# The second gate and the second up projection as three fp32r matmuls over split operands

## The chip, the cores and the metric

The kernel runs as one program on one core of a Trainium2 chip. The metric is device microseconds of one execution. Three timed runs of the kernel before gave 1217.91, 1217.97 and 1218.64 us, median 1217.97. One further execution was profiled, and all rows below are from that one. The chip's engines are named as the profile names them: PE (TensorE matmuls) and PEld (its weight loads), DVE (VectorE), ACT (ScalarE), POOL (GpSimd) and SP (SyncE, which here issues nearly all DMAs).

## The reference, cut to what matters

One layer over 256 tokens of width 1024, with 16 meta tokens set ahead of them. A mixer with an attention branch and a state space branch is followed by a mixture of 32 experts, each token to its best 4.

```python
g_a = jax.nn.sigmoid(proj[..., GA_OFF:GB_OFF])      # proj = h @ w_in
g_b = jax.nn.sigmoid(proj[..., GB_OFF:IN_COLS])
merged = g_a * (y_a @ w_up_a) + g_b * (y_b @ w_up_b)
return merged @ w_o
...
for e in range(N_EXPERTS):
    gate = jnp.minimum(t @ w_gate[e] + b_gate[e], SWIGLU_LIMIT)
    up = jnp.clip(t @ w_up[e] + b_up[e], -SWIGLU_LIMIT, SWIGLU_LIMIT)
    act = (up + 1.0) * gate * jax.nn.sigmoid(SWIGLU_ALPHA * gate)
    out = out + comb[:, e:e + 1] * (act @ w_down[e] + b_down[e])
```

g_b is the second gate (1024 x 1024 weights, 272 rows of h of which 256 count), y_b @ w_up_b the second up projection (512 x 1024 weights). All inputs are float32. The experts' three matrices are 12 MB each expert, 384 MB in all.

## The kernel before, in words

The work falls into a front (norm, projections, attention, scan, gates, output projection, router) and the expert loop, which goes over 16 pairs of experts. The order of PE and of SP is that of the program text (a manual schedule); the order of ACT, DVE and POOL is written by a planner that simulates the program and takes, among the instructions that it holds for ready, the one of highest priority. `tc.high_priority` raises that priority.

Weights come in tiles of 1 MB (128 partitions x 2048 float32). In the front they go through pool `wA` (6 tiles), and two further pools, `wC` and `wB`, are laid over memory that the front gives back: `wC` over that of the attention, `wB` over that of the scan. A fixed list, `slots` (20 homes; the first round, `first`, has 21), says into which home each quarter matrix of an expert goes. SP issues the loads in that order and waits at each one until the home's last reader is done. `prefetch(n)` issues the next n of them ahead of the expert loop. So at the start of the expert loop up to 21 MB of weights lie in SBUF, and from then on each load waits for a home to be used up.

`project` (line 214) is 8 matmuls of a 128 x 128 weight piece against 256 columns of hT, in float32. `gate_tile(i, hf_, j)` calls it for gate i, half hf_ and column block j, and ACT puts the result through tanh (L744). `up` (L764) is 4 such matmuls. The order of the front on PE around the change is: gate 0 (8 tiles), the up projection `up_a` d = 0 to 3, gate 1 tiles (0, 0) and (0, 1), up_a 4 and 5, gate 1 tiles (0, 2) and (0, 3), up_a 6 and 7, gate 1 tiles (1, 0) to (1, 3), the glu projection (4 times `up`), 32 transposing matmuls of hT into the output sums (L832), `up` of w_up_b for d = 0 to 7, then the output projection (L935) for the first and second half of the tokens, the latter mixed with the router, and the first gather. Two DVE instructions for each d (L839, L840) turn up_b's sums into mT, which the output projection reads.

The experts' gate and up biases are split into three bfloat16 pieces: rows are loaded three times (`braw`, six DMAs, L788), copied to `bias` by ACT (L789), and three times subtracted by DVE and copied by ACT (L792, L793), over all 2048 columns at once. The experts' loop uses them at L1064, and the home `acc` is the memory of `braw`.

Of the kernel before, what the change touches and what calls it, by code (L numbers as in the profile page):

```python
# [30 lines left out]
NS = 64  # L31
NPAIR = NG // 2
NE = 32
NWA, NWB, NWC = 6, 7, 5
NLEV = 9
HP = 120
CH = T // 2
# [11 lines left out]
def hybrid_trunk_kernel(ctx: ExitStack, tc: tile.TileContext, x, meta, ln_in_g, ln_in_b, w_in, b_f,  # L49
# [47 lines left out]
    def slab(src, kt):  # L97

        n = src.shape[1]
        src = src.rearrange("(k p) n -> p k n", p=P)  # L100
        nk, ks = 2048 // n, []
        for k0 in range(0, kt, nk):
            v_ = wA.tile([P, 2048], F32, name="w", tag="w").rearrange("p (k n) -> p k n", n=n)
            nc.sync.dma_start(v_, src[:, k0:k0 + nk])
            ks += [v_[:, k] for k in range(nk)]
        return ks

    def wslice(c0):
        return slab(w_in[0, :, c0:c0 + 512], KD)
# [101 lines left out]
    def project(w, j, n0, n1):  # L211
        pt = pst(n1 - n0)
        for k in range(KD):
            TE.matmul(pt, w[k][:, j * P:(j + 1) * P], hT[:, k, n0:n1], start=k == 0, stop=k == KD - 1)  # L214
        return pt
# [474 lines left out]

    moe = ExitStack()
    wC = moe.enter_context(tc.tile_pool(name="wC", bufs=NWC, reuse_waits="tile"))
    pools = {"wA": wA, "wC": wC, "fk": fk, "keep": keep}
    ready = {}
    nload = [0]
    slots = [("wC", "w")] * NWC + [("wB", "w")] * (NWB - 4) + [("wA", "w")] * NWA + [("keep", "gate1")]
    slots += [("wB", "w")] * 4 + [("fk", "hT")]
    first = slots[:NWC + NWB + NWA - 3] + [("keep", "acc")] + slots[NWC + NWB + NWA - 3:]

    def homes():  # L700

# [29 lines left out]
    def prefetch(n):  # L731
        seq = [(w, e, qtr) for e in range(2) for w in (w_gate, w_up) for qtr in range(4)]
        seq += [(w_down, e, qtr) for qtr in range(4) for e in range(2)]
        for _ in range(n):
            w, e, qtr = seq[nload[0]]
            ready[(w.tensor.name, e, qtr)] = expert_load(w, e, qtr)
# [3 lines left out]

    gate = [keep.tile([P, KD, SEQ], F32, name=f"gate{i}", tag=f"gate{i}") for i in range(2)]

    def gate_tile(i, hf_, j):
        S.activation(gate[i][:, 4 * hf_ + j], project(wg[2 * i + hf_], j, NMETA, T), AF.Tanh, scale=0.5)  # L744

    gate_tile(0, 0, 0)
    scan_out(5)
# [7 lines left out]
    scan_out(6)  # L755
    gate_tile(0, 1, 2)
    gate_tile(0, 1, 3)
    wg.append(wslice(GB_OFF))
    prefetch(2)

    def up(w, y, d):
        pt = pst(SEQ)
# [10 lines left out]
    scan_out(7)  # L773
    up_a(2)
    up_a(3)
    wg.append(wslice(GB_OFF + 512))
    scan.close()
    bp = moe.enter_context(tc.tile_pool(name="bp", bufs=1, side="right"))
    mk = front.enter_context(tc.tile_pool(name="mk", bufs=2, side="right"))
# [6 lines left out]
    for j, src in enumerate((b_gate, b_up)):  # L786
        for g in range(3):
            nc.sync.dma_start(braw[NE * g:NE * g + NE, j], src[0])  # L788
    S.copy(bias, braw)  # L789
    for g in (1, 2, 2):  # L790
        gs = slice(NE * g, NE * g + NE)
        V.tensor_tensor(braw[gs], braw[gs], bias[gs], ALU.subtract)  # L792
        S.copy(bias[gs], braw[gs])  # L793
    pick = keep.tile([3 * NE, NE], BF16, name="pick")
    with nc.allow_low_precision(reason="sums of zeros and a one"):
        V.tensor_reduce(pick, ident[:3 * NE, :3 * NE].rearrange("p (b e) -> p e b", e=NE), AX.X, ALU.add)
# [14 lines left out]
    for j in range(4):  # L811
        gate_tile(1, 1, j)
    prefetch(NWB - 4)
    wub = slab(w_up_b[0], 4)


    bh = mk.tile([P, 4], F32, name="bh")
# [1 line left out]
    for j in range(4):  # L819
        pt = up(wg_, y2T, j)  # L820
        tg = mk.tile([P, SEQ], F32, name="tg", tag="tg")
        S.activation(tg, pt, AF.Tanh, scale=0.25, bias=bh[:, j:j + 1])
        V.scalar_tensor_tensor(ybT[:, j], tg, 1.0, y2T[:, j], op0=ALU.add, op1=ALU.mult)


    po = [pw.tile([P, 2, 512], F32, name="po", tag="po"), [pst(512), pst(512)]]
# [5 lines left out]
            TE.matmul(pt, hT[:, k, ts], ident, start=k % 4 == 0, stop=False, skip_group_check=True)  # L832

    mT = fk.tile([P, KD, SEQ], F32, name="mT", tag="hT")
    prefetch(NWA)
    for d in range(KD):
        pt = up(wub, ybT, d)
        m2 = mk.tile([P, SEQ], F32, name="m2", tag="m2")
        V.scalar_tensor_tensor(m2, gate[1][:, d], 1.0, pt, op0=ALU.add, op1=ALU.mult)  # L839
        V.scalar_tensor_tensor(mT[:, d], m2, 0.125 / ALPHA, gate[0][:, d], op0=ALU.mult, op1=ALU.add)  # L840
# [178 lines left out]
    def weights(p, sel):  # L1019
        V.tensor_mul(sel, sel, bc(comb[:, :, 2 * p:2 * p + 2], 3, CAP))  # L1020
        pt = px.tile([P, 512], F32, name="px", tag="px")
        for i in range(2):
            TE.transpose(pt[:, i * P:(i + 1) * P], sel[:, i].rearrange("p e s -> p (e s)"), ident)
        selT = mp.tile([P, SEQ], F32, name="selT", tag="selT", bufs=2)
        S.copy(selT, pt[:, :SEQ])
        if p + 1 == NE // 2:

            pt = px.tile([P, 512], F32, name="px", tag="px")
            for i in range(2):
                for g in range(2):  # L1030
                    TE.matmul(pt[64 - 64 * g:128 - 64 * g, i * P:(i + 1) * P], sel[:, i, g], ident,
                              start=True, stop=True, skip_group_check=True)
            selX.append(mp.tile([P, SEQ], F32, name="selX"))
            S.copy(selX[0], pt[:, :SEQ])
        return selT

# [112 lines left out]
    def crowded():  # L1149

        anyc = nc.values_load(cnti[0:1, NE:NE + 1], min_val=0, max_val=SEQ)
        with tc.If(anyc > CAP):  # L1152
# [1 line left out]
            for s_ in home[nload[0] - 8:nload[0]]:  # L1154
                free.remove(s_)
            free = [s_ for s_ in free if s_[0] != "keep"]
            free.sort(key=lambda s_: ("wC", "fk", "wB", "wA").index(s_[0]))

            def slot(n):
                pool, tag = free[n]  # L1160
# [8 lines left out]
            with tc.For_i(0, NE, 1) as e:  # L1169
                ce = nc.values_load(cnti[0:1, bass.ds(e, 1)], min_val=0, max_val=SEQ)  # L1170
                with tc.If(ce > CAP):
                    def weights_of(w, n):
                        ts = []
                        for qtr in range(4):
                            ts.append(slot(n + qtr).rearrange("p (k n) -> p k n", n=D))
                            nc.gpsimd.dma_start(ts[-1], w[0, bass.ds(e, 1), qtr * 256:qtr * 256 + 256]
                                              .rearrange("o (k p) n -> p (o k) n", p=P))
                        return ts

                    scr = slot(1)  # L1180
                    a, sg, br, bu = scr[:, 0:512], scr[:, 512:1024], scr[0:1, 1024:], scr[32:33, 1024:]
                    nc.gpsimd.dma_start(br, b_gate[0, bass.ds(e, 1), :])
                    nc.gpsimd.dma_start(bu, b_up[0, bass.ds(e, 1), :])
                    aT = slot(2).rearrange("p (k t) -> p k t", k=KD)
                    wg_e, wu_e = weights_of(w_gate, 3), weights_of(w_up, 7)
                    for i in range(2):
                        for n in range(2):
                            ns = slice(n * 512, n * 512 + 512)
                            pts = []
                            for ws, bb_, r, tag in ((wg_e, br, 0, "pg"), (wu_e, bu, 32, "pu")):  # L1190
                                pt = pg.tile([P, 512], F32, name=tag, tag=tag)
                                TE.matmul(pt, ones[r:r + 1, 0:P], bb_[:, ns], start=True, stop=False)
                                for k in range(KD):
                                    TE.matmul(pt, h1Td[:, k, i * P:(i + 1) * P], ws[k // 2][:, k % 2, ns],
                                              start=False, stop=k == KD - 1)
                                pts.append(pt)
                            V.tensor_scalar_min(a, pts[0], 7.0)
                            S.activation(sg, a, AF.Sigmoid, scale=1.702)
                            V.tensor_mul(sg, sg, a)
                            V.tensor_scalar(a, pts[1], 7.0, -7.0, op0=ALU.min, op1=ALU.max)  # L1200
                            V.scalar_tensor_tensor(a, a, 1.0, sg, op0=ALU.add, op1=ALU.mult)
                            pt = px.tile([P, 512], F32, name="px", tag="px")
                            for j in range(4):
                                TE.transpose(pt[:, j * P:(j + 1) * P], a[:, j * P:(j + 1) * P], ident)
                            V.tensor_copy(aT[:, 4 * n:4 * n + 4, i * P:(i + 1) * P],
                                          pt.rearrange("p (k t) -> p k t", k=4))
                    wd_e = weights_of(w_down, 7)
                    for i in range(2):
                        for n in range(2):
                            ns = slice(n * 512, n * 512 + 512)  # L1210
                            pt = px.tile([P, 512], F32, name="px", tag="px")
                            for k in range(KD):
                                TE.matmul(pt, aT[:, k, i * P:(i + 1) * P], wd_e[k // 2][:, k % 2, ns],
                                          start=k == 0, stop=k == KD - 1)
                            V.scalar_tensor_tensor(acc[:, i, ns], pt, over[:, i, bass.ds(e, 1)], acc[:, i, ns],
                                                   op0=ALU.mult, op1=ALU.add)
# [147 lines left out]
```

## Time and profile before

| | before |
|---|---|
| median of 3 runs (lowest, highest) | 1217.97 us (1217.91, 1218.64) |
| the profiled execution: time, span of its instructions | 1219.16 us, 1217.6 us |
| mean granted TensorE clock over the span | 0.983 |
| PE busy, DVE busy, ACT busy | 1123.3, 334.8, 177.1 us |
| read from HBM | 431.64 MB, mean 355 GB/s over the span |

A profile is read in slices of time. [...] A timeline row has the start in us, the length from the start of the first to the end of the last instruction that it merges, the engine, the line of the kernel, the operation with out<-in, the shapes and the count; idle time before it and what ended it stand in brackets. Matmuls are pipelined and each one's length includes the way through the array, so the pace of a stream is read from the start of one row to the start of the next.

### The profile page before, as it was taken

What the parts mean: (1) busy time and instruction counts of PE and PEld (TensorE: products, weight loads), DVE (VectorE), ACT (ScalarE), POOL (GpSimd) and SP (SyncE); (2) the same over time, 40 slices, a digit from 0 to 9 for tenths busy, and PEclk for the clock granted to TensorE, in tenths of its full rate; (3) what the DMA queues carried; (4) which work ended last, traced back from release to release, by engine and by line L of the source; (5) the groups of instructions that cost most, each with busy time, mean ns of one, the idle gap of its engine ahead of it and who ended that gap; (6) DMA issues with size and microseconds to landing.
All of it is one profiled execution on the core that took longest, in us unless ns stands there. A gap on an engine that the chain in (4) does not pass through costs nothing. (4 is left out here: it accounts for less than half of the span.)

```text
span 1217.6 us, 13190 instructions
## 1 busy us (share of the span) xinstructions
PE 1123.3 (92%) x5398; PEld 579.7 (48%) x5399; DVE 334.8 (27%) x781; ACT 177.1 (15%) x387; POOL 59.0 (5%) x115
## 2 busy tenths in 40 slices
PE   4889999998999999999999999988999899988994
PEld 2778788853545444443444353424343344333431
DVE  3969422233121212111131312121212121212003
ACT  2257403021101011010101010101010111000000
POOL 3333200000000000000000000000000000000001
PEclk9999999998999999999999999999999999999998
DMA  7743289557999999999999999999999999999993
GB/s 151 187 103 71 105 206 385 229 205 303 392 421 420 421 421 421 421 421 409 421 421 421 421 421 421 421 421 420 421 420 421 422 421 421 421 421 421 421 421 129
DMA packets 75674, 433.59 MB, mean 356 GB/s; under 512 B 14219, under 2 KB 14571, under 8 KB 26587
## 3 DMA queue, kind: packets, MB, share of 16 engines
q1 hardware_dynamic: 75178, 432.19, 89.6%
q8 instruction: 44, 0.72, 0.2%
q10 hardware_dynamic: 432, 0.52, 0.1%
q14 instruction: 20, 0.16, 0.0%
HBM read 431.64 MB, written 1.05 MB: 355 GB/s over the span
## 5 line engine op out<-in xcount | busy, mean ns | idle before, releaser
L1061 PE MATMUL pu<-w,xy 128*64 128x512 f32 x1024 | 237.9, 595 | 13.3 <-DMA w<-in_w_up_dram 13.2
L1061 PE MATMUL pg<-w,xy 128*64 128x512 f32 x1024 | 236.3, 594 | 4.0 <-PEq L1152 2.3
L1093 PE MATMUL Yp<-w,aT 128*64 128x512 f32 x960 | 227.0, 609 | 0.0
L1061 PEld LDWEIGHTS pu<-w,xy 128*64 128x64 f32 x1024 | 80.6, 136 | 154.5 <-issue 110.0
L1061 PEld LDWEIGHTS pg<-w,xy 128*64 128x64 f32 x1024 | 85.1, 137 | 142.0 <-issue 133.4
L1093 PEld LDWEIGHTS Yp<-w,aT 128*64 128x64 f32 x960 | 94.1, 140 | 121.3 <-issue 106.0
L214 PE MATMUL ps<-hT,w 128*128 128x256 f32 (+1 forms) x512 | 119.3, 392 | 2.8 <-ACT pr L595 2.8
L214 PEld LDWEIGHTS ps<-hT,w 128*128 128x128 f32 x512 | 98.0, 194 | 19.7 <-ACT pr L595 3.1
L1071 DVE TENSOR_SCALAR pg<-pg 128x512 f32<-128x512 f32 x32 | 22.4, 700 | 232.0 <-PE pg L1064 232.0
L1072 ACT ACTIVATE ups<-pg 128x512 f32<-128x512 f32 x32 | 19.1, 597 | 413.9 <-DVE pg L1071 413.9
L1074 DVE TENSOR_SCALAR pu<-pu 128x512 f32<-128x512 f32 x32 | 22.4, 700 | 189.8 <-PE pu L1064 189.8
L1096 DVE COPY xy<-Yp 128x512 f32<-128x512 f32 x15 | 10.4, 692 | 222.6 <-PE Yp L1093 222.6
L1123 PE MATMUL px<-xy,selT 128*128 128x512 f32 x112 | 57.7, 636 | 4.5 <-DVE acc L1125 2.4
L944 PE MATMUL px<-sel,z 128*128 128x128 f32 x480 | 59.8, 283 | 0.6 <-DVE sel L949 0.6
L944 PEld LDWEIGHTS px<-sel,z 128*128 128x128 f32 x480 | 58.6, 196 | 0.8 <-ACT aT L1083 0.8
L1322 POOL TENSOR_TENSOR acc<-acc,gb 128x512 f32<-128x512 f32 (+1 forms) x2 | 2.4, 1216 | 1050.3 <-ACT acc L1320 1050.3
L1097 ACT COPY xy<-Yp 128x512 f32<-128x512 f32 x15 | 8.8, 585 | 217.2 <-PE Yp L1093 217.2
L1083 ACT COPY aT<-px 128x512 f32<-128x512 f32 x32 | 18.7, 586 | 134.5 <-PE px L1081 134.5
L1123 PEld LDWEIGHTS px<-xy,selT 128*128 128x128 f32 x112 | 19.1, 194 | 39.8 <-DVE acc L1125 18.1
L1125 DVE TENSOR_TENSOR acc<-acc,px 128x512 f32<-128x512 f32 x52 | 34.7, 684 | 11.6 <-PE px L1123 11.5
L884 DVE TENSOR_SCALAR xy<-px,pcolP 128x128 f32<-128x128 f32 x60 | 23.7, 410 | 45.4 <-ACT xy L886 43.4
L886 ACT ACTIVATE xy<-px,pcolP 128x128 f32<-128x128 f32 x60 | 25.8, 455 | 44.6 <-PE px L944 42.6
(407 smaller groups left out, 831.5 us busy)
## 6 DMA issues: line engine op xcount, KB each, us to landing
w<-in_w_gate_dram SPq DMA_DIRECT2D x128, 1024.0 KB
w<-in_w_up_dram SPq DMA_DIRECT2D x128, 1024.0 KB
w<-in_w_down_dram SPq DMA_DIRECT2D x127, 1024.0 KB
w<-in_w_in_dram SPq DMA_DIRECT2D x16, 1024.0 KB
w<-in_w_o_dram SPq DMA_DIRECT2D x4, 1024.0 KB
w<-in_w_up_a_dram SPq DMA_DIRECT2D x2, 1024.0 KB
w<-in_w_up_b_dram SPq DMA_DIRECT2D x2, 1024.0 KB
w<-in_w_glu_dram SPq DMA_DIRECT2D x1, 1024.0 KB
```

The source lines that it names most:

```text
L214: TE.matmul(pt, w[k][:, j * P:(j + 1) * P], hT[:, k, n0:n1], start=k == 0, stop=k == KD - 1)
L884: V.tensor_scalar(out_, in_, g_, b_, op0=ALU.mult, op1=ALU.add)
L886: S.activation(out_, in_, AF.Identity, scale=g_, bias=b_)
L944: TE.matmul(pts[k // 4][:, (k % 4) * P:(k % 4 + 1) * P], z1[:, i, paired(k)], sel[:, i].rearrange("p e s -> p (e s)"), start=i == 0 and k ...
L1061: TE.matmul(pt[64 * n:64 * n + 64], XT[:, kk, c0:c0 + CAP], wt[:, k, n * 512:n * 512 + 512], start=kk == 0, stop=False, skip_group_check=True)
L1071: V.tensor_scalar_min(pgt, pgt, 7.0)
L1072: S.activation(up, pgt, AF.Sigmoid, scale=1.702)
L1074: V.tensor_scalar(put, put, 7.0, -7.0, op0=ALU.min, op1=ALU.max)
L1083: S.copy(aT.rearrange("p j h s -> p (j h s)"), pt)
L1093: TE.matmul(Yp[n][64 * g:64 * g + 64], aTs[g][:, j, half], wd[g][:, k, n * 512:n * 512 + 512], start=qtr == 0 and k == 0, stop=qtr == 3 an ...
L1123: TE.matmul(pt, selT[:, i * P:(i + 1) * P], Ysb[:, ns], start=True, stop=True)
L1125: V.tensor_add(acc[:, i, ns], acc[:, i, ns], pt)
```

## The change

The change has four parts. (1) The 8 tiles of the second gate and the 8 of the second up projection are computed by a new `three_passes`. For each piece of weights ACT copies the float32 values into an fp32r tile `whs` (the high half), DVE subtracts that from the original into an fp32r tile `wls` (the low half), and PE multiplies high by high, high by low and low by high, with 256 moving columns. The pieces rotate over four quarters of `whs` and `wls`. (2) The moving operand is split likewise: hT into `hTh` and `hTl` ahead of the second gate, ybT into `ybh` and `ybl` (in the same memory) in the glu loop. (3) The memory for this comes from the pools: `wC` 5 to 2, `wB` 7 to 6, and the four new tiles become homes for expert weights once they have been used, so that `slots` and `first` keep 20 and 21 entries; the prefetches are 2, 2 and 10 where they were 2, 2, 3 and 6, with the rest behind the output projection in both. (4) The bias pieces are made in four chunks of 512 columns. The loads of the second gate and of w_up_b keep their sizes, and the crowded path, which did not run, is only reordered.

```diff
-NWA, NWB, NWC = 6, 7, 5
+NWA, NWB, NWC = 6, 6, 2
...
+    def gslice(c0):
+        src = w_in[0, :, c0:c0 + 512].rearrange("(k p) n -> p k n", p=P)
+        vs = []
+        for k0 in (0, 4):
+            vs.append(wA.tile([P, 2048], F32, name="w", tag="w").rearrange("p (k n) -> p k n", n=512))
+            nc.sync.dma_start(vs[-1], src[:, k0:k0 + 4])
+        return vs
...
+    wX = moe.enter_context(tc.tile_pool(name="wX", bufs=1, reuse_waits="tile"))
...
-    slots = [("wC", "w")] * NWC + [("wB", "w")] * (NWB - 4) + [("wA", "w")] * NWA + [("keep", "gate1")]
-    slots += [("wB", "w")] * 4 + [("fk", "hT")]
-    first = slots[:NWC + NWB + NWA - 3] + [("keep", "acc")] + slots[NWC + NWB + NWA - 3:]
+    slots = [("wC", "w")] * NWC + [("wB", "w")] * (NWB - 4) + [("wA", "w")] * NWA + [("wX", "whs"), ("wX", "wls")]
+    slots += [("wX", "hTl"), ("fk", "hTh"), ("keep", "gate1")] + [("wB", "w")] * 4 + [("fk", "hT")]
+    first = slots[:-5] + [("keep", "acc")] + slots[-5:]
...
+    whs = wX.tile([P, 4, 512], F32R, name="whs", tag="whs")
+    wls = wX.tile([P, 4, 512], F32R, name="wls", tag="wls")
+    piece = [0]
+    def three_passes(ws, j, high, low):
+        pt = pst(SEQ)
+        k0, kt = 0, sum(v_.shape[1] for v_ in ws)
+        i = piece[0] % 4
+        for h_, v_ in enumerate(ws):
+            nk = v_.shape[1]
+            if h_ == 0 or nk == 4:
+                i = piece[0] % 4
+                piece[0] += 1
+            at = (k0 % 4) * P
+            wh, wl = (t_[:, i, at:at + nk * P].rearrange("p (k n) -> p k n", n=P) for t_ in (whs, wls))
+            v_ = v_[:, :, j * P:(j + 1) * P]
+            with tc.high_priority(offset=HP):
+                S.copy(wh, v_)
+                V.tensor_sub(wl, v_, wh.bitcast(F32))
+            for k in range(nk):
+                kk = k0 + k
+                TE.matmul(pt, wh[:, k], high[:, kk], start=kk == 0, stop=False)
+                TE.matmul(pt, wh[:, k], low[:, kk], start=False, stop=False)
+                TE.matmul(pt, wl[:, k], high[:, kk], start=False, stop=kk == kt - 1)
+            k0 += nk
+        return pt
     def gate_tile(i, hf_, j):
-        S.activation(gate[i][:, 4 * hf_ + j], project(wg[2 * i + hf_], j, NMETA, T), AF.Tanh, scale=0.5)
+        if i:
+            pt = three_passes(wg[2 + hf_], j, hTh[:, :, NMETA:], hTl[:, :, NMETA:])
+        else:
+            pt = project(wg[hf_], j, NMETA, T)
+        S.activation(gate[i][:, 4 * hf_ + j], pt, AF.Tanh, scale=0.5)
...
-    wg.append(wslice(GB_OFF))
-    prefetch(2)
+    wg.append(gslice(GB_OFF))
+    hTh = fk.tile([P, KD, T], F32R, name="hTh", tag="hTh")
+    hTl = wX.tile([P, KD, T], F32R, name="hTl", tag="hTl")
+    for k in range(0, KD, 2):
+        S.copy(hTh[:, k:k + 2], hT[:, k:k + 2])
+        V.tensor_sub(hTl[:, k:k + 2], hT[:, k:k + 2], hTh[:, k:k + 2].bitcast(F32))
...
-    S.copy(bias, braw)
-    for g in (1, 2, 2):
-        gs = slice(NE * g, NE * g + NE)
-        V.tensor_tensor(braw[gs], braw[gs], bias[gs], ALU.subtract)
-        S.copy(bias[gs], braw[gs])
+    for j in range(2):
+        for n in range(2):
+            ns = slice(n * 512, n * 512 + 512)
+            S.copy(bias[:, j, ns], braw[:, j, ns])
+            for g in (1, 2, 2):
+                gs = slice(NE * g, NE * g + NE)
+                V.tensor_tensor(braw[gs, j, ns], braw[gs, j, ns], bias[gs, j, ns], ALU.subtract)
+                S.copy(bias[gs, j, ns], braw[gs, j, ns])
...
-    wub = slab(w_up_b[0], 4)
+    wub = []
+    for i in range(2):
+        wub.append(wA.tile([P, 2048], F32, name="w", tag="w").rearrange("p (k n) -> p k n", n=D))
+        nc.sync.dma_start(wub[-1], w_up_b[0, 256 * i:256 * i + 256].rearrange("(k p) n -> p k n", p=P))
+    ybh = fk.tile([P, 4, SEQ], F32R, name="ybh", tag="hTh")
+    ybl = wX.tile([P, 4, SEQ], F32R, name="ybl", tag="hTl")
...
         V.scalar_tensor_tensor(ybT[:, j], tg, 1.0, y2T[:, j], op0=ALU.add, op1=ALU.mult)
+        S.copy(ybh[:, j], ybT[:, j])
+        V.tensor_sub(ybl[:, j], ybT[:, j], ybh[:, j].bitcast(F32))
...
-    prefetch(NWA)
+    prefetch(4 + NWA)
     for d in range(KD):
-        pt = up(wub, ybT, d)
+        pt = three_passes(wub, d, ybh, ybl)
...
-            selX.append(mp.tile([P, SEQ], F32, name="selX"))
+            selX.append(mp.tile([P, SEQ], F32, name="selX", tag="sel", bufs=1))
```

## Rows read from the trace of the kernel before

**Rows 1.** The page, span in 40 slices: DMA share in tenths, and rate.
```profile
DMA  7743289557999999999999999999999999999993
GB/s 151 187 103 71 105 206 385 229 205 303 392 421 420 421 421 421 421 421 409 421 421 421 421 421 421 421 421 420 421 420 421 422 421 421 421 421 421 421 421 129
```

**Rows 2.** Windows: length, busy PE, PEld, DVE, ACT, POOL, clock, DMA share, GB/s.
```profile
180.00:225.00 45.00, 45.00 (x226) 40.01 (x225) 9.96 (x11) 12.34 (x16) 0.00 (x0) 1.00 1.02 375
225.00:285.00 60.00, 56.01 (x229) 35.47 (x229) 23.36 (x85) 9.78 (x19) 0.00 (x0) 0.94 0.44 162
285.00:1200.00 915.00, 865.51 (x4040) 379.08 (x4038) 180.84 (x307) 81.70 (x162) 0.00 (x0) 0.99 1.01 417
```

**Rows 3.** Timeline of SP's DMA issues; a merged row's length includes the waits inside it.
```profile
199.85 20.93 SPq L728 DMA_DIRECT2D w<-in_w_gate_dram  x4
236.97 2.35 SPq L728 DMA_DIRECT2D w<-in_w_up_dram  x4
255.00 31.80 SPq L728 DMA_DIRECT2D w<-in_w_down_dram  x8
288.19 5.70 SPq L728 DMA_DIRECT2D w<-in_w_gate_dram  x4
```

**Rows 4.** Timeline of PE, from the second gate to the first expert.
```profile
178.81 7.07 PE L214 MATMUL ps<-hT,w 128*128 128x256 f32 x32
199.53 13.98 PE L214 MATMUL ps<-hT,w 128*128 128x256 f32 x64
213.35 7.07 PE L764 MATMUL ps<-y2T,w 128*128 128x256 f32 x32
220.25 1.95 PE L832 MATMUL po<-ident,hT 128*128 128x128 f32 x16
222.04 1.95 PE L832 MATMUL ps<-ident,hT 128*128 128x128 f32 x16
223.82 13.98 PE L764 MATMUL ps<-ya__1272,w 128*128 128x256 f32 x64
237.64 13.90 PE L935 MATMUL po<-w,mT 128*128 128x512 f32 x32
259.12 1.87 PE L899 MATMUL ps<-wrg,z1T 128*128 128x32 f32 x16
260.82 3.68 PE L935 MATMUL ps<-w,mT 128*128 128x512 f32 x8
268.04 1.88 PE L935 MATMUL ps<-w,mT 128*128 128x512 f32 x4
281.06 7.09 PE L1061 MATMUL pg<-w,xy 128*64 128x512 f32 x32 [0.49 <-ACT xy L886]
287.98 0.39 PE L1064 MATMUL pg<-bias,pick 96*64 96x512 bf16 x2
288.20 7.04 PE L1061 MATMUL pu<-w,xy 128*64 128x512 f32 x32
```

**Rows 5.** Groups of instructions by shape: count | busy us, mean ns | idle before, releaser.
```profile
L1083 ACT COPY aT<-px 128x512 f32<-128x512 f32 x32 | 18.7, 586 | 134.5 <-PE px L1081 134.5
L1073 DVE TENSOR_TENSOR ups<-ups,pg 128x512 f32<-128x512 f32 x32 | 22.0, 687 | 21.2 <-ACT ups L1072 21.2
L1025 ACT COPY selT<-px 128x256 f32<-128x256 f32 x16 | 6.0, 372 | 5.8 <-PE px L1023 5.8
L1020 DVE TENSOR_TENSOR sel<-sel,comb 128x256 f32<-128x256 f32 x16 | 6.8, 425 | 0.0
L744 ACT ACTIVATE gate<-ps 128x256 f32<-128x256 f32 x16 | 6.0, 382 | 36.1 <-PE ps L214 36.0
L839 DVE SCALAR_TENSOR_TENSOR m<-gate,ps 128x256 f32<-128x256 f32 x8 | 3.4, 421 | 10.3 <-PE ps L764 10.3
```

**Rows 6.** Timeline of ACT: the bias copy that waits for its DMA.
```profile
188.10 1.90 ACT L789 CAST bias<-braw 96x2048 bf16<-96x2048 f32 x1 [10.30 <-DMA braw<-in_b_up_dram]
```

More of the change, by code (lines that the diff above doesn't have):

```diff
@@ L692, in hybrid_trunk_kernel @@
     wC = moe.enter_context(tc.tile_pool(name="wC", bufs=NWC, reuse_waits="tile"))
-    pools = {"wA": wA, "wC": wC, "fk": fk, "keep": keep}
+    wX = moe.enter_context(tc.tile_pool(name="wX", bufs=1, reuse_waits="tile"))
+    pools = {"wA": wA, "wC": wC, "wX": wX, "fk": fk, "keep": keep}
     ready = {}
     nload = [0]
-    slots = [("wC", "w")] * NWC + [("wB", "w")] * (NWB - 4) + [("wA", "w")] * NWA + [("keep", "gate1")]
-    slots += [("wB", "w")] * 4 + [("fk", "hT")]
-    first = slots[:NWC + NWB + NWA - 3] + [("keep", "acc")] + slots[NWC + NWB + NWA - 3:]
+    slots = [("wC", "w")] * NWC + [("wB", "w")] * (NWB - 4) + [("wA", "w")] * NWA + [("wX", "whs"), ("wX", "wls")]
+    slots += [("wX", "hTl"), ("fk", "hTh"), ("keep", "gate1")] + [("wB", "w")] * 4 + [("fk", "hT")]
+    first = slots[:-5] + [("keep", "acc")] + slots[-5:]
     def homes():
@@ L775, in hybrid_trunk_kernel @@
     up_a(3)
-    wg.append(wslice(GB_OFF + 512))
+    wg.append(gslice(GB_OFF + 512))
     scan.close()
@@ L1156, in crowded @@
             free = [s_ for s_ in free if s_[0] != "keep"]
-            free.sort(key=lambda s_: ("wC", "fk", "wB", "wA").index(s_[0]))
+            free.sort(key=lambda s_: ("wC", "wX", "fk", "wB", "wA").index(s_[0]))
             def slot(n):
@@ L1171, in crowded, with weights_of @@
                 with tc.If(ce > CAP):
-                    def weights_of(w, n):
-                        ts = []
+                    def weights_of(w, ts):
                         for qtr in range(4):
-                            ts.append(slot(n + qtr).rearrange("p (k n) -> p k n", n=D))
-                            nc.gpsimd.dma_start(ts[-1], w[0, bass.ds(e, 1), qtr * 256:qtr * 256 + 256]
-                                              .rearrange("o (k p) n -> p (o k) n", p=P))
+                            nc.gpsimd.dma_start(ts[qtr], w[0, bass.ds(e, 1), qtr * 256:qtr * 256 + 256]
+                                                .rearrange("o (k p) n -> p (o k) n", p=P))
                         return ts
@@ L1184, in crowded @@
                     aT = slot(2).rearrange("p (k t) -> p k t", k=KD)
-                    wg_e, wu_e = weights_of(w_gate, 3), weights_of(w_up, 7)
+                    tg_, tu_ = ([slot(n + qtr).rearrange("p (k n) -> p k n", n=D) for qtr in range(4)] for n in (3, 7))
+                    wg_e, wu_e = weights_of(w_gate, tg_), weights_of(w_up, tu_)
                     for i in range(2):
@@ L1206, in crowded @@
                                           pt.rearrange("p (k t) -> p k t", k=4))
-                    wd_e = weights_of(w_down, 7)
+                    wd_e = weights_of(w_down, tu_)
                     for i in range(2):
```

## The prediction

> **What bounds the kernel now.** I read the span in slices first. From the eleventh slice on the DMA engines move about 420 GB/s to the last but one; before that the rate changes from slice to slice [rows 1]. The windows say the same: from 285 us the DMA share is 1.01 while PE is busy for 865 of 915 us, and from 225 to 285 it is the other way round, with a DMA share of 0.44 and PE busy for 56 of 60 us at the full clock level for nearly all of it [rows 2]. So the expert loop is bound by its loads, and its end is fixed by when the unbroken stream begins. A tile of 1.049 MB at 417 GB/s is 2.5 us. The last slice moved 129 GB/s x 30.4 us = 3.9 MB, so the stream ends near 1196.5 and a tail of some 21 us follows.
>
> The next question is what starts the stream. SP's timeline has the loads from 199.85 on in few, long rows, because they wait for homes; the row of eight that begins at 255.0 reaches into the expert loop, with the next load issued only at 288.19 [rows 3]. PE starts the first expert at 281.06 [rows 4]; eight matmul records later, at 282.8, the first home is free. Ahead of that the DMA engines stand still for about 0.56 x 60 = 34 us [rows 2]: they are full, not slow. Hence each microsecond that PE's front gives back moves the first expert, the stream and the end by one microsecond, as long as 21 tiles still lie ready when the first expert starts.
>
> PE's pace in the changed stages is read from starts. The last four tiles of the second gate run from 199.53 to 213.35, 3.455 us a tile; the eight steps of up_b from 223.82 to 237.64, 1.73 us a step [rows 4]. A float32 matmul leaves two records: 8 matmuls of a tile are 16 records (64 for four tiles), each 0.216 us for 256 columns.
>
> **The matmuls.** Removed: 8 x 3.455 = 27.6 and 8 x 1.73 = 13.8, together 41.5 us of PE. Added: 8 tiles x 8 blocks of k x 3 and 8 steps x 4 blocks x 3 = 288 fp32r matmuls of 256 columns. The trace has no fp32r matmul, so its pace p is bounded by rows. From below: a weight load. The L899 group has only 32 moving columns and 128 x 128 weights, and 16 of its records go by from 259.12 to 260.82, 0.106 us each; the load sets that pace [rows 4]. From above: 0.216, a float32 record of 256 columns. Nearest is the L832 group: a 128 x 128 load and a stream that is also about 0.107 us long (half the columns of a 0.216 us record), 16 of them in 1.79 us, 0.112 each, so the two overlap [rows 4]. That the stream of 256 columns in fp32r is as short as that is the assumption. What speaks for it is bf16: the two L1064 matmuls of 512 columns, on two halves of the array at once, take 0.22 us (287.98 to 288.20), while a pair of float32 matmuls of that shape leaves four L1061 records of 0.216 us, 0.865 us, four times as long [rows 4]. I take p = 0.112: 288 x 0.112 = 32.3 us, 9.2 us less than before. At 0.106 it is 10.9 less, at 0.144 nothing, at 0.216 it is 20.7 more.
>
> [...]
>
> **The splits.** A gate tile needs two pieces of 512 columns: 2 x 0.586 on ACT by a copy of that shape, plus a tanh of 0.382, 1.55 us; 2 x 0.687 on DVE, 1.37 us [rows 5]. PE's new tile is 24 x 0.112 = 2.69 us, so PE stays the slowest and four quarters of buffer let the splits run two tiles ahead. In up_b a step needs two pieces of 256 columns: 2 x 0.372 on ACT, and on DVE 2 x 0.425 plus the two instructions that were there (0.42 each), 1.69 us against PE's 12 x 0.112 = 1.34 [rows 5]. There DVE is slower, but four steps are split ahead during the glu and the transposes (10 us), and from then on DVE has 4 x 0.85 + 8 x 0.84 = 10.1 us to PE's 10.7. I count nothing; without that lead it would cost 8 x 0.35 = 2.8 us. The output projection begins with mT's first block, so a late last block costs nothing either. The copies of hT (4 pieces on each engine, 544 columns) lie between 140 and 178 us, where ACT and DVE are mostly idle; those of ybT end some 2 us after the glu, under the transposes' 3.6 us [rows 4]. If that cover went, the price would be these 2 us.
>
> **The bias pieces.** Chunks make 16 ACT copies and 12 DVE subtractions of 512 columns, at most 16 x 0.586 = 9.4 and 12 x 0.687 = 8.2 us [rows 5]. Nothing in the front waits for them, since they are first used behind the first expert's gate [rows 4] and their memory is a home filled only after the last up_b step. But ACT and DVE work in order, and the splits now queue among them. Before, ACT's first bias copy stood for 10.3 us until 188.1, because its DMA came late, with a tanh queued behind it [rows 6]. A split stuck there is one that PE waits for. The third gate tile starts at 178.81 + 2 x 2.69 + 3.45 = 187.6. If its first piece stands behind one chunk that waits to 188.1, the low half is ready at 188.1 + 0.59 + 0.59 + 0.69 = 190.0 and PE loses 2.4 us; if the planner has put it ahead, nothing. I take the middle, 1.2. From 188 to the end of the gates at 208.4 ACT has 9.4 + 7.0 (12 pieces) + 3.1 (8 tanh) = 19.5 us for 20.3, and DVE 8.2 + 8.2 + 1.7 = 18.1: it fits, with little room.
>
> **The loads.** Three tiles fewer are fetched ahead of w_up_b, and ten instead of six after it. What counts is when the 21st is in. New times: gates end at 208.4, glu at 215.3, transposes at 218.9, up_b at 229.6. By then eight tiles of the list (2, 2 and four of wA, which wait for wg and glu) are in, as the DMA has 34 us of slack there [rows 2]. wA's last two, the four split tiles, gate1 and acc are eight loads, from 229.6 to about 250. The four wo homes and hT come free with the output projection, the last 32 us behind the end of up_b as before (237.64 to 269.9) [rows 4], at 261.9. Two loads later, at 267, all lie ready. The first expert starts at 281.1 - 8.0 = 273.1, its first home is free at 274.8. So the stream starts with the list full, with 8 us to spare, and the whole gain goes through. Homes in the loop are 20 as before, in the same order of use. The larger fk pool and selX move memory only.
>
> **The sum.** The profiled execution took 1219.16 us, 1.56 more than its span. 1219.16 - 9.2 + 1.2 = 1211.2. It lies 1.2 us above the median of the three runs, so the forecast is 1210.0 against 1217.97.
>
> **Rivals.**
> (a) Loads that don't hide under the stream, or fp32r at float32's pace: slower. Place: every matmul of the two stages. Then p = 0.106 + 0.107 = 0.213, or 0.216, and the front grows by 20 us: 1238. It decides from p = 0.144 on. Against it stands the L832 group, where full-array loads and streams of that very length run at 0.112 [rows 4]; for it, that no row shows fp32r. Chance 0.09. [...]
> (b) The splits set the pace: PE waits for ACT and DVE among the bias chunks. For it: the 19.5 us of 20.3, and the wait to 188.1 [rows 6]. Against: the splits' raised priority and two tiles of lead. If ACT and DVE overlapped only half, 28 us from 188 on, the gates would end at 216 instead of 213.35 [rows 4], up_b's 3.1 us would make that good, and the time be 1217.5; fully in turn, 37.6 us, 1227. It turns slower where a gate tile takes more than 3.455 us. Chance 0.17: 0.07 for half the gain left (1213 to 1215), 0.06 for none, 0.04 for slower.
> (c) The list isn't full when the first expert starts. Each tile missing costs 2.5 us of stream. With 8 us to spare it takes four tiles to lose anything much; two more than that leave 1215. For it: seven early tiles became four. Chance 0.06, still faster, at about 1213.
>
> **How the numbers follow.** The forecast's own case has 0.68, from 1207 (p at 0.106, no wait) to 1213 (p = 0.120, 2.4 us of waits). A measurement of this kernel can tell 0.2%, 2.4 us, from no change. Faster than 1215.5: 0.68 + 0.07 of (b) + 0.06 of (c) = 0.81; within: 0.06; slower: 0.09 + 0.04 = 0.13. The range reaches from 1207 to 1216; above it lie (a) and the last two parts of (b), 0.19 together, and below it hardly anything, since 0.106 is a floor for p.
>
> **What would show it.** Right: a gate tile every 2.7 us and an up_b step every 1.35 us by starts, PE without waits on ACT or DVE but for one near 188, the first expert near 273, the stream unbroken from 275. Wrong: a pace of 0.2 us a matmul; many short waits of PE on `whs` or `wls`; DMA share near 1 right up to the first expert, which would mean the list was not full; or a first expert that moved while the end did not.

## The result and the profile after

The changed kernel is slower: 1228.26 us median of six runs (1226.20 to 1229.30) against 1218.41 us for the kernel before, measured beside it. The ratio is 1.0075, with a 95% interval from 1.0064 to 1.0086. The forecast was 1210.0 us with a range of 1207 to 1216, so it had the wrong sign, and the time lies 12 us above the range.

| | before | after |
|---|---|---|
| median | 1218.41 us | 1228.26 us |
| the profiled execution: time, span | 1219.16, 1217.6 us | 1226.20, 1224.6 us |
| second gate starts | 178.81 us | 179.65 us |
| first expert starts | 281.06 us | 282.12 us |
| load 128, the rows of b_down, issued (loads counted from 0) | 538.25 us | 538.16 us |
| last load of an expert matrix issued (row begins) | 1177.78 us | 1186.21 us |

The last three rows of the table split the loss. The front, forecast to be 8 us shorter, is 1.1 us longer. By load 128 the two kernels are level again; from there to the last load 8.5 us are lost, where nothing was forecast. Behind the last load the changed kernel is 1.4 us shorter. The two profiled executions lie 7.0 us apart, the medians 9.85, so one trace of each doesn't account for all of the difference.

The page of the changed kernel, DMA share in tenths and rate over 40 slices, answers to [rows 1]:

```profile
DMA  7742369577999999999999989999999999999993
GB/s 146 190 101 38 138 137 371 226 288 308 414 421 420 422 420 421 421 421 408 393 423 389 421 359 422 420 422 419 421 421 421 421 421 421 420 421 422 420 421 154
```

Before, only one slice of the stream stood clearly under 420 GB/s, that with the rows of b_down (409, and 408 here). Now 393, 389 and 359 follow it, in every second slice (a slice is 30.6 us). The windows of the same stretches, answering to [rows 2] (length, busy PE, PEld, DVE, ACT, POOL, granted clock, DMA share, GB/s):

```profile
180.00:225.00 45.00, 40.23 (x265) 38.03 (x264) 24.03 (x44) 24.92 (x51) 0.00 (x0) 0.92 0.88 311
225.00:285.00 60.00, 55.99 (x286) 37.78 (x286) 26.17 (x95) 12.38 (x28) 0.00 (x0) 0.97 0.64 246
285.00:1200.00 915.00, 858.99 (x4014) 371.70 (x4011) 181.21 (x308) 82.27 (x161) 0.00 (x0) 0.99 1.00 416
```

PE now stands still for 4.8 of the 45 us from 180 on, at a mean clock of 0.92; before it never stood still there. The timeline of PE, answering to [rows 4], shows where; the idle time before a matmul and what ended it stand in brackets:

```profile
179.65 0.47 PE L775 MATMUL ps<-hTh,whs 128*128 128x256 f32 x1
185.50 3.62 PE L811 MATMUL ps<-ya__1272,w 128*128 128x256 f32 x16
191.62 0.39 PE L775 MATMUL ps<-hTh,whs 128*128 128x256 f32 x1 [2.51 <-ACT whs L771]
191.84 0.28 PE L776 MATMUL ps<-hTl,whs 128*128 128x256 f32 x1
194.38 0.58 PE L777 MATMUL ps<-hTh,wls 128*128 128x256 f32 x1 [2.25 <-DVE wls L772]
194.76 0.42 PE L775 MATMUL ps<-hTh,whs 128*128 128x256 f32 x1
194.97 0.41 PE L776 MATMUL ps<-hTl,whs 128*128 128x256 f32 x1
217.29 7.07 PE L811 MATMUL ps<-y2T,w 128*128 128x256 f32 x32
227.68 0.36 PE L775 MATMUL ps<-ybh,whs 128*128 128x256 f32 x1
239.18 13.90 PE L992 MATMUL po<-w,mT 128*128 128x512 f32 x32
282.12 7.15 PE L1118 MATMUL pg<-w,xy 128*64 128x512 f32 x32 [0.49 <-ACT xy L943]
```

The first two tiles take 5.85 us (179.65 to 185.50). Then PE waits for the high half of the next piece and right after it for the low half, and goes on at 0.21 us a matmul instead of 0.12. Windows around this place give the clock:

```profile
189.00:191.60 2.60, 0.11 (x1) 0.00 (x0) 2.47 (x5) 2.38 (x5) 0.00 (x0) 1.00 1.04 414
191.60:194.40 2.80, 0.52 (x3) 0.32 (x3) 2.67 (x5) 2.73 (x5) 0.00 (x0) 0.85 1.02 405
194.40:200.50 6.10, 6.10 (x29) 6.10 (x30) 5.52 (x9) 5.93 (x12) 0.00 (x0) 0.51 0.93 341
```

While PE stands, ACT and DVE are busy for nearly all of it; after the two waits PE runs for 6 us at a granted clock of 0.51. ACT's timeline, answering to [rows 6], and one row of DVE's show what they were busy with:

```profile
187.28 1.14 ACT L839 CAST bias<-braw 96x512 bf16<-96x512 f32 x2 [8.46 <-DMA braw<-in_b_up_dram]
189.15 1.14 ACT L839 CAST bias<-braw 96x512 bf16<-96x512 f32 x2 [0.74 <-DMA braw<-in_b_up_dram]
190.31 0.62 ACT L843 CAST bias<-braw 32x512 bf16<-32x512 f32 x1
190.95 0.62 ACT L771 CAST whs<-w 128x512 fp32r<-128x512 f32 x1
191.60 1.26 ACT L843 CAST bias<-braw 32x512 bf16<-32x512 f32 x2
192.88 0.62 ACT L771 CAST whs<-w 128x512 fp32r<-128x512 f32 x1
187.93 5.67 DVE L842 TENSOR_TENSOR braw<-braw,bias 32x512 f32<-32x512 f32 x8 [7.46 <-ACT bias L839]
```

ACT stands before the first bias chunk until 187.3. All four first copies and one of the later ones come ahead of the split that PE waits for (190.95), and nothing else does. On DVE eight subtractions of bias chunks come ahead of the low half.

SP's rows, answering to [rows 3], show that the list was full as forecast (eight loads in a row up to the expert loop, and the next one only at 289.32):

```profile
240.11 2.16 SPq L738 DMA_DIRECT2D w<-in_w_up_dram  x4
256.54 31.39 SPq L738 DMA_DIRECT2D w<-in_w_down_dram  x8
289.32 5.70 SPq L738 DMA_DIRECT2D w<-in_w_gate_dram  x4
```

The loop's loss, in windows of the changed kernel:

```profile
600.00:650.00 50.00, 46.91 (x232) 22.53 (x228) 14.77 (x25) 4.81 (x10) 0.00 (x0) 1.00 0.98 405
650.00:700.00 50.00, 46.51 (x208) 17.53 (x208) 11.02 (x17) 2.02 (x4) 0.00 (x0) 1.00 0.97 401
700.00:750.00 50.00, 43.05 (x202) 17.40 (x198) 8.22 (x16) 4.45 (x9) 0.00 (x0) 1.00 0.93 383
```

At 421 GB/s, which the kernel before had in all three, the missing 16, 20 and 38 GB/s are 1.9, 2.4 and 4.5 us of stream, 8.8 us, near the 8.5 of the table. SP's issues of one such set of eight loads, first after, then before, show the loads waiting (20 us of stream need no more than 20 us of issue):

```profile
682.34 33.53 SPq L738 DMA_DIRECT2D w<-in_w_down_dram  x8
```

```profile
680.08 17.74 SPq L728 DMA_DIRECT2D w<-in_w_down_dram  x8
```

The place of these breaks fits one item of the list. In pair 5 the rows of b_down take the home that is next, at load 128, place (128 - 21) mod 20 = 7 of `slots`, and keep it until pair 9. Before, place 7 was a tile of `wB`; with the new list it is one of `wA`. In the list `wA` has six places in a row, so with five tiles left the sixth load of each row has to wait until the tile of the first, five loads back, has been read. SP's waits for PE from 590 to 790 us show this (total, times, longest):

```profile
SPq L738 <- PE Yp L1150: 19.8, 2, 11.1
SPq L738 <- PE pg L1118: 7.9, 1, 7.9
SPq L738 <- PE pu L1118: 5.6, 1, 5.6
```

These are four waits, for the matmuls that read gate weights (`pg`), down weights (`Yp`, twice) and up weights (`pu`). Just such tiles stand five loads ahead of loads 150, 170, 190 and 210, the sixth `wA` load of four rounds, and these are the loads that are late. Load 189 and load 190, for one, were issued 21 us apart:

```profile
693.55 21.37 SPq L738 DMA_DIRECT2D w<-in_w_down_dram  x2
```

In the kernel before, no wait of SP for PE in that stretch is longer than this one:

```profile
SPq L728 <- PE pu L1061: 0.3, 1, 0.3
```

### The profile page after: what moved, and what is told of

It is laid out like the page before. It is cut to its first block, busy times and chain, and to the rows that moved or that the text cites. A ratio compares the mean times of both kernels' runs of the same rounds, so it can differ in the third digit from the quotient of the medians.

```text
span 1224.6 us, 13516 instructions
## 1 busy us (share of the span) xinstructions
PE 1118.1 (91%) x5494; PEld 574.6 (47%) x5495; DVE 357.0 (29%) x830; ACT 197.9 (16%) x439; POOL 58.9 (5%) x115
## 5 line engine op out<-in xcount | busy, mean ns | idle before, releaser
L1150 PE MATMUL Yp<-w,aT 128*64 128x512 f32 x960 | 223.3, 598 | 1.8 <-DMA w<-in_w_down_dram 1.8
L1118 PEld LDWEIGHTS pu<-w,xy 128*64 128x64 f32 x1024 | 78.0, 136 | 162.2 <-issue 107.3
L223 PE MATMUL ps<-hT,w 128*128 128x272 f32 (+1 forms) x384 | 92.2, 399 | 2.8 <-ACT pr L604 2.8
L223 PEld LDWEIGHTS ps<-hT,w 128*128 128x128 f32 x384 | 74.4, 197 | 16.7 <-ACT pr L604 3.2
```

What stands on the lines that cost most here:

```text
L1118: TE.matmul(pt[64 * n:64 * n + 64], XT[:, kk, c0:c0 + CAP], wt[:, k, n * 512:n * 512 + 512], start=kk == 0, stop=False, skip_group_check=True)
L1150: TE.matmul(Yp[n][64 * g:64 * g + 64], aTs[g][:, j, half], wd[g][:, k, n * 512:n * 512 + 512], start=qtr == 0 and k == 0, stop=qtr == 3 an ...
```

## The experiments

Theory A: two separate losses. In the front the splits stand in ACT's and DVE's order behind bias chunks whose DMA lands late; in the loop b_down's rows sit in a `wA` home. The rivals: (B) the new homes themselves break the stream, or the splits are too slow by themselves; (C) it is the amount of bias work, not the late DMA. The ratio of each kernel is to the kernel before, run beside it.

**b_down's rows in a wB home.**

```diff
-        if p == 5:
-            bdown = [load_rows(b_down[0])]
-        elif p in (6, 7):
+        if p in (6, 7):
...
         upB = activate(1, *gate_up(2 * p + 1, norm_rows if p == 12 else None))
+        if p == 5:
+            bdown = [load_rows(b_down[0])]
```

> The changed kernel with one line moved: the row load of b_down is issued half a pair later (after the second expert's gate and up of pair 5), so that it takes home 15 of the list, a wB tile, instead of home 7, a wA tile. Theory A (b_down's rows keep one of six wA tiles for four pairs, so the last wA home of each round waits for the first of the same round, five loads back, and the stream breaks): the DMA share from 600 to 750 us goes from 0.98, 0.97, 0.93 back to about 1.01 and the time falls by 6 to 9 us, to 1219 to 1222. Rival B (the four new homes whs, wls, hTl, hTh break the stream): no change, 1228, share under 1 in the same stretches. The first expert still starts at 282 under both.

Measured: 1219.67 us median, ratio 1.0001 (0.9989 to 1.0012), from 1.0075: 9 us less. The same three windows:

```profile
600.00:650.00 50.00, 48.47 (x237) 22.41 (x233) 12.41 (x19) 2.37 (x4) 0.00 (x0) 1.00 1.01 421
650.00:700.00 50.00, 46.62 (x213) 19.95 (x213) 12.82 (x23) 4.46 (x9) 0.00 (x0) 1.00 1.01 421
700.00:750.00 50.00, 46.67 (x216) 20.79 (x212) 11.18 (x20) 4.45 (x9) 0.00 (x0) 1.00 1.01 422
```

The stream is whole with all four new homes in the list, so rival B falls. SP still waits for PE, up to 8.1 us at a time from 590 to 790 us, since the held tile is missing in `wB` now; but the six places of `wB` don't stand in a row, and the DMA share shows no loss by these waits. PE's two waits in the front are still there (2.6 and 2.2 us). In this execution the first expert started at 285.54, not 282, because the clock was 0.89 from 90 to 120 us, ahead of everything that the change touches, where the changed kernel's execution had 1.00; the second gate started at 183.44 us for 179.65.

**The kernel before with b_down's rows in a wA home.** The same edit with `if p == 4`, in the kernel before: place 11 of its list.

> The kernel before with one line moved: b_down's rows are loaded half a pair earlier (after the second expert of pair 4), so that they take home 11 of its list, a wA tile, instead of home 7, a wB tile. Theory A: the stream breaks once a round until pair 9, DMA share 0.93 to 0.98 in some stretches of 550 to 750 us, time up by 6 to 10 us to 1224 to 1228, with no fp32r and no new home in the kernel. Rival B (the new homes do it): no change, 1218.

Measured: 1234.69 us, ratio 1.0117 (1.0090 to 1.0143), 15 us more. Three of its windows:

```profile
550.00:600.00 50.00, 48.25 (x232) 22.01 (x229) 11.17 (x19) 5.05 (x10) 0.00 (x0) 1.00 0.91 372
700.00:750.00 50.00, 44.83 (x220) 19.43 (x218) 6.84 (x12) 5.05 (x10) 0.00 (x0) 1.00 0.96 396
750.00:800.00 50.00, 45.82 (x198) 20.28 (x196) 10.93 (x20) 3.86 (x8) 0.00 (x0) 0.93 0.85 349
```

The loss appears without any fp32r. It is larger than expected; the home is held for half a pair longer and the breaks fall elsewhere, but what of the size is due to which was not tried.

**The bias chunks behind the gates.**

```diff
     for j in range(4):
-        gate_tile(1, 1, j)
+        gmark = gate_tile(1, 1, j)
+    with tc.issue_after(gmark.ins):
+        ...   # the bias chunks, moved here
```

> The changed kernel with the bias chunks' ACT and DVE work ordered behind the last gate tile's tanh; the DMAs of braw stay where they are. Theory A (the splits stand behind bias copies that wait for their DMA, PE waits 4.9 us and then runs at the lower clock level for 6 us): both waits and the slow stretch go, the gates end near 209.5 instead of 217.3, the first expert starts near 274.5 and the time falls by 6 to 8 us, to 1220 to 1222. Rival B (PE's waits come from the splits themselves, ACT and DVE being too slow): the waits stay and the time falls by under 2 us.

Measured: 1232.67 us, ratio 1.0113 (1.0087 to 1.0138): no gain, but 4 us more than the changed kernel. The waits in the gates were gone, but others came in the next stage. PE's waits from 170 to 290 us, total, times and longest:

```profile
PE ps L775 <- ACT ybh L880: 3.5, 2, 2.8
PE ps L776 <- DVE ybl L881: 1.4, 1, 1.4
```

The chunks now stood, with nothing to wait for, in the glu loop ahead of the splits of ybT (`ybh`, `ybl`), and cost the same 4.9 us there. So theory A's reading of the wait as a matter of the late DMA alone doesn't hold for this place: the bulk of bias work ahead of a split is enough. Of the 4 us that this kernel is slower than the changed one, the traces show 1.0 at the first expert (283.15 us for 282.12) and some 1.5 in the loop (DMA share 0.95 for 0.98 from 600 to 650 us); what makes up the rest is open.

**braw loaded early.**

```diff
     wua = slab(w_up_a[0], 4)
+    braw = ...   # its tile and its six DMAs, moved here from behind the wB pool
```

> The changed kernel with the six DMAs of braw issued right behind the load of w_up_a, some 30 us earlier; the bias chunks keep their place in the program. If the late landing is the cause (theory A): no bias copy waits for a DMA, PE's waits shrink from 4.9 to under 1 us, no slow stretch, time 1220 to 1222, like the run that puts the chunks behind the gates. If it is the amount of bias work on ACT and DVE among the splits (theory C): the waits remain at 2 us or more and less than half the gain is there, 1224 or above.

Measured: 1219.78 us, ratio 1.0005 (0.9994 to 1.0017), 8.5 us less than the changed kernel. PE had no wait from 175 to 240 us, and the first expert began nearly 8 us earlier:

```profile
274.34 7.35 PE L1118 MATMUL pg<-w,xy 128*64 128x512 f32 x32 [0.49 <-ACT xy L943]
```

ACT's first bias row shows what changed:

```profile
179.11 2.18 ACT L839 CAST bias<-braw 96x512 bf16<-96x512 f32 x4 [0.61 <-DVE y2T L534]
```

Rival C falls for this place: the same chunks stay in the same order among the splits of the same tiles, and cost nothing once none of them waits. They start 8 us earlier (179.11 for 187.28), in time in which ACT had stood still, so that the splits queued among them are ready when PE comes to them. Together with the run before this says that a split is late either way, behind a wait or behind much work, if it has no such lead. The breaks in the loop were still there (DMA share 0.98, 0.98 and 0.93 from 600 to 750 us).

**Both mends.** braw early, and b_down's rows at pair 7 (`if p == 7`, ahead of the residual), place 15, a `wB` tile in this list, and held for two pairs.

> The changed kernel with both mends: braw loaded behind w_up_a, and b_down's rows loaded at pair 7, where their home is a wB tile and is needed for two pairs only. Theory A (two separate losses, one in the front and one in the loop, which add up): first expert near 274.3 as with braw early alone, DMA share 1.01 through 600 to 750 us, time 1210 to 1213, that is 6 to 9 us under the kernel before. Rival: the loop gives the front's gain back in some other place (the stream is bound by PE in part), time 1215 to 1219.

Measured: 1211.94 us, ratio 0.9936 (0.9924 to 0.9948). From 1.0075 that is 17 us less; the two mends by themselves gave 9.0 and 8.5, so they add up. Start of the second gate, start of the output projection, first expert, and the window of the former breaks:

```profile
178.59 0.47 PE L775 MATMUL ps<-hTh,whs 128*128 128x256 f32 x1
230.19 13.89 PE L992 MATMUL po<-w,mT 128*128 128x512 f32 x32
273.60 7.27 PE L1118 MATMUL pg<-w,xy 128*64 128x512 f32 x32 [0.50 <-ACT xy L943]
```

```profile
600.00:750.00 150.00, 141.32 (x652) 61.65 (x650) 37.85 (x63) 11.28 (x22) 0.00 (x0) 0.99 1.01 418
```

This kernel beats both: 7.2 us under the kernel before.

**The same two edits in the kernel before.**

> The kernel before with the same two edits (braw early, b_down's rows at pair 7) and no fp32r. Theory A: nothing in the kernel before waited for either, so 1217 to 1220, no change by more than 0.2%; then the gain of both_mended is that of the fp32r passes. Rival: the mends are worth something by themselves, 1210 to 1215.

Measured: 1219.02 us, ratio 0.9998 (0.9989 to 1.0007). Neither edit is worth anything without the fp32r passes, so the 7.2 us are theirs.

**Gates only.** With both mends, w_up_b's projection back in float32:

```diff
-        pt = three_passes(wub, d, ybh, ybl)
+        pt = up(wubk, ybT, d)
```

> The kernel with both mends, with w_up_b's projection back in float32 (8 times 1.73 us, no split of ybT); only the gate stays in three passes. Theory A: up_b's part is 13.8 less 11.5 us as the changed kernel's trace has it, so 2.3 us more than with both, 1213 to 1215, and the first expert near 276.6. Rival: up_b's gain is eaten by DVE, no difference.

Measured: 1213.31 us, ratio 0.9946 (0.9933 to 0.9959). The first expert starts 2.6 us later than with both mends:

```profile
276.16 7.78 PE L1115 MATMUL pg<-w,xy 128*64 128x512 f32 x32 [0.50 <-ACT xy L940]
```

The trace bears out the 2.3 us; in the times the difference is 1.4 us, and the intervals overlap.

**Whole bias pieces.** With both mends, the bias made over 2048 columns at once, as before the change.

> The kernel with both mends, with the bias pieces made over all 2048 columns at once as in the kernel before (ACT 1.9 us, DVE 2.3 us each). If the chunks matter (theory D): the splits stand behind 1.9 us copies, PE waits 1 to 4 us between 185 and 200 and the time is 1212 to 1216. If they don't once the DMA is early (theory E): as with both mends, 1210 to 1213.

Measured: 1212.38 us, ratio 0.9944 (0.9932 to 0.9956), as with chunks, and PE without a wait. ACT shows the long copies between the splits:

```profile
184.04 1.90 ACT L840 CAST bias<-braw 32x2048 bf16<-32x2048 f32 x1
185.97 1.14 ACT L771 CAST whs<-w 128x512 fp32r<-128x512 f32 x2
```

Four quarters of buffer cover a copy of 1.9 us. The chunks, the fourth part of the change, are worth nothing that these runs can tell, with braw early; whole pieces behind the late DMA were not tried together with the splits.

## Why the prediction was wrong

**What bounds the kernel** was right. Where the first expert started 7.8 us earlier (braw early) the time fell by 8.5 us, and in the kernel before and the changed one the 21 loads of the list were issued before the first expert began: the row of eight had its fifth load, the 21st, out by 270.8 and 272.3 us.

**The matmuls**: right in kind, the size a little off. From the second gate to the output projection the kernel with both mends needs 230.19 - 178.59 = 51.6 us. Taking off what did not change (four pairs of up_a and glu steps, 13.8, and the transposes, 3.6) leaves 34.2 us for 288 matmuls, p = 0.119 where 0.112 was taken. The saving is 7.3 us instead of 9.2. So 256 columns of fp32r with a weight load of their own go by at 0.119 us, where a float32 matmul of that shape takes 2 x 0.216 us; 0.119 is nearly the pace of the L832 group, 0.112 [rows 4], and rival (a), p = 0.213, is contradicted.

**The splits** by themselves were rightly counted at nothing: with both mends PE has no wait in either stage, up_b included. In the changed kernel PE did wait for them among the bias chunks, the place that rival (b) named, and the gates ended at 217.29 where 208.4 was forecast. But (b) priced it as ACT and DVE not keeping up from 188 us on, and braw early shows that they do keep up once no chunk waits.

**The bias pieces**: the first step that failed, in its size. The mechanism was named, a split stuck behind a chunk whose DMA is late, with at most 2.4 us and a middle of 1.2. The trace shows 4.9 us of waits (2.51 + 2.25 and the gaps beside them) and some 2.5 us more, because PE's clock then fell to 0.51 and about 27 matmuls took 0.21 us each instead of 0.12. The bound of 2.4 allowed for one chunk ahead of the split and a split that then passes at once. In fact five ACT copies came ahead of it, and eight DVE subtractions ahead of its low half, and the fall of the clock was not priced at all.

**The loads**: the step that failed outright was "Homes in the loop are 20 as before, in the same order of use", and with it "the stream starts with the list full ... and the whole gain goes through". The count was the same, the order of the pools was not: place 7, which b_down's rows hold for four pairs, had become a tile of `wA`, and the sixth `wA` load of each round then waited. That cost 9 us. Rival (c) looked at the same list, but only up to the first expert.

With the two failed steps mended the time is 1211.94 us, 0.6% under the kernel before, inside the range. The forecast's sum lacked 9 us in the loop and 6 in the front (7.4 for 1.2), and its saving was 1.9 us too large; that is 17 of the 18.3 us between 1210.0 and 1228.26. Of the rest, 0.8 us stand ahead of the change, since the second gate started at 179.65 where 178.81 was taken.

## What to carry to other kernels

When a change reorders a list of buffers, look up what lands in each place through the whole loop, above all anything that is held for longer than a round; a pool of n tiles with n places in a row has no slack once one is held (here 9 us). Work that nothing waits for wasn't free on ACT and DVE, which took their instructions in the order written: splits stood behind bias chunks in the changed kernel and with the chunks behind the gates, and PE waited 4.9 us each time. So ask what will be queued behind its DMA wait and behind the work itself, and load its operand so early that it has none and is done before the queued work is needed. A gain in the front of a stream-bound kernel is worth its full size only if the stream stays whole behind it: here 7.2 us with it whole, and nothing with its breaks (ratio 1.0005 with braw early).

## What was unexpected in the hardware's numbers

An fp32r matmul of 256 columns shows as one record and goes by at 0.119 us, each with its own 128 x 128 load, where the same float32 matmul leaves two records of 0.216 us. ACT's copy to fp32r of 128 x 512 takes 0.62 us (a float32 copy of that shape out of the matmul sums 0.586 [rows 5]). Two waits of 2.65 and 2.3 us with two matmuls between them were followed by 6 us at a granted clock of 0.51, and that cost half as much again as the waits. And executions of one kernel differ by 4.5 us (1217.19 to 1221.69 for the kernel before, in one set of runs); in two profiled ones (b_down's rows in a wB home, and the kernel before with them in a wA home) the clock was 0.89 from 90 to 120 us, where in those of the kernel before, the changed kernel and both mends it was 1.00, and the second gate started at 183.44 and 183.57 us, where it was 178.59 to 179.65 in those three.
